# FFN gate and up as 2 by 2 blocks in seven products, inner features in chunks of 6, partial sums through DRAM

## The chip, the core and the metric

The kernel runs on one NeuronCore of a Trainium2 chip, as one launch. The metric is the time of that launch on the device in microseconds (us); of several runs the median is given.

## What is computed

A bidirectional encoder of two layers with a width of 1024 over 256 + 512 = 768 tokens, all in float32. Each layer has three token mixers (SSD, GLA, attention) with gates, an output projection and a residual, and then a gated FFN with 2816 inner features. The change is in the FFN and just ahead of it:

```python
def _layer(x, ...):
    h = _rmsnorm(x, norm1_w)
    proj = h @ w_in          # 12 parts: z, xbc, dt, gla q/k/v/..., attention q/k/v, gates
    ...
    merged = (g[:, :, 0] * (o_ssd @ w_br_ssd)
              + g[:, :, 1] * (o_gla @ w_br_gla)
              + g[:, :, 2] * (o_att @ w_br_attn))
    x = x + merged @ w_out
    h2 = _rmsnorm(x, norm2_w)
    gate, up = _split(h2 @ w_ffn_in, (D_FF, D_FF))
    return x + (jax.nn.silu(gate) * up) @ w_ffn_out
```

## The kernel before

Activations lie transposed: a tile has 128 features in the partitions and all T = 768 tokens in the columns; 8 such tiles are the width of 1024. Float32 precision comes from two parts of each operand: `hi`, rounded by ScalarE to the matmul type fp32r, and `lo`, the rest, by a subtraction. A product is three matmuls, hi x hi, hi x lo and lo x hi. Each weight unit of 512 columns (4 blocks of 128 x 128) is loaded by a DMA on SyncE's queue and split by `wunit` (L617): `hi` on ScalarE, `lo` on the engine `lo_eng`, which is VectorE from the SSD output projection to the end of the layer and GpSimd elsewhere. There are 3 buffers for raw units and 5 each for `hi` and `lo`.

`gemm_a` (L628) makes a block of 128 output features for all tokens: for each of the `kt` input blocks it runs the three products on two halves of HT = 384 tokens, so 6 matmuls for each input block and 48 for a width of 1024. The last input block comes after all the others, so that its activations may come late. The sum stands in a PSUM tile of two banks, of which there are two.

The FFN (L924 to L966) goes through 22 blocks of 128 inner features, in chunks of 8, 8 and 6 (`FF_CHUNKS`, L27). For block j it runs `gemm_a` for the gate ("fg"), multiplies by the row's rstd `r2`, applies Silu, runs `gemm_a` for up ("fu"), multiplies, and splits the result into `hid` (hi and lo). After a chunk the down projection "fo" runs `gemm_a` over the chunk's blocks for each of the 8 output blocks m and adds into `xa[m]`, which stays in SBUF from the first chunk to the last. In the last layer the last block goes through `finish` (L968) in two token halves, with the final norm.

Ahead of the FFN (L885 to L921): SSD output times z gate gives `yz` (tiles `ea`, two buffers, and `ld`, one). Six of the eight "g0" gate projections run early (`early_gate`, L1015) and go through DRAM, the last two inside `gate_branch` (L1023). The output projection "wo" (L913) adds the residual and makes `x2`, split into hi and lo.

The order of instructions is written out ahead of time: `Plan.schedule` (L450) is a list scheduler with costs that keeps each engine's stream in one fixed order. An operation recorded under `first()` goes ahead of the others that are ready. Operations of GpSimd, and those of VectorE that touch SBUF alone, are planned so that they exclude each other (`op.port`, L349). SBUF beyond the fixed tiles is cut into cells that the phases of a layer share in turn (`phase`, L603). All instructions are emitted on one line, L574, so the profile's groups go by operation and shape.

## Time and profile before

| | us |
|---|---|
| median of 3 runs | 3123.14 |
| lowest and highest | 3118.91, 3123.22 |
| the profiled execution | 3119.5 |
| its span in the profile | 3117.7 |

The profile names engines PE (TensorE matmuls), PEld (weight loads), DVE (VectorE), ACT (ScalarE), POOL (GpSimd) and SPq (SyncE's queue of DMA issues). base_S and cell are SBUF, base_P is PSUM, wts the weights and d_x, d_z, d_g and the like tensors in DRAM.

A group of instructions shows engine, operation, output <- inputs, shapes and count, then busy time in us and the mean of one in ns, then the idle time of the engine just before them with what ended it. A timeline line shows the start, the duration, the engine and the operation, and in brackets the idle time before it. A window shows for its stretch the busy time (and count) of PE, PEld, DVE, ACT and POOL in us, then PE's granted clock as a share of the full one, the share of the DMA engines and GB/s.

The FFN of layer 0 runs from about 1016 to 1564 us, that of layer 1 from about 2552 to 3101 us.

### The profile page before, as it was taken

Reading aid. Unit: us, or ns where it says so; the run is one execution under the profiler, and the core shown is the slowest. Engines: PE = TensorE matmul, PEld = TensorE weight load, DVE = VectorE, ACT = ScalarE, POOL = GpSimd, SP = SyncE. Lnnn points to the kernel's source line nnn. Section 1 sums busy time; section 2 is a strip of 40 time slices with the busy share of each in tenths; the row PEclk is TensorE's granted clock in tenths of the full one; section 3 lists DMA queues with packets and bytes.
Section 4 is the critical chain, followed back from the end, with each engine's and each line's share of the span. In section 5 each row is a group of like instructions: output and inputs, shape, how many; then the busy total and the mean of one; then the engine's idle time right before and its main releaser. Section 6 shows DMA issues by size and latency. Waiting matters only on the chain.

```text
span 3117.7 us, 46591 instructions
## 1 busy us (share of the span) xinstructions
PE 3041.2 (98%) x18160; PEld 2983.5 (96%) x18160; DVE 1606.6 (52%) x2737; ACT 1205.3 (39%) x2109; POOL 992.1 (32%) x972
## 2 busy tenths in 40 slices
PE   8999999999999999999999999999999999999998
PEld 7989989999899999999999899999998999999998
DVE  4766576856533333333447656776765333333233
ACT  4666454433323221212346755543333232122123
POOL 4533555655252000000164244556543410000002
PEclk8999999999999999999999999999999999999999
DMA  3233223444545222222222332334335452222222
GB/s 108 61 79 114 90 88 110 127 114 112 173 134 178 66 61 65 65 61 65 89 76 70 77 120 85 98 110 131 118 99 182 128 165 65 61 65 64 62 61 68
DMA packets 200012, 301.32 MB, mean 97 GB/s; under 512 B 17584, under 2 KB 90672, under 8 KB 199792
## 3 DMA queue, kind: packets, MB, share of 16 engines
q1 hardware_dynamic: 199792, 298.35, 31.8%
q8 instruction: 143, 2.34, 0.3%
q14 instruction: 77, 0.63, 0.1%
HBM read 246.18 MB, written 52.10 MB: 96 GB/s over the span
## 4 chain that ended last, share of the span: by engine, by line
PE 62%; DVE 3%; ACT 1%; DMA 0%; issue 0%; POOL 0%; DVEq 0%; ACTq 0%; POOLq 0%
PE base_P L574 62%; DVE cell L574 3%; ACT cell L574 1%; DVE base_S L574 0%; DMA base_S<-wts 0%; ACT L574 0%; ACT base_S L574 0%; DMA base_S<-d_z 0%; DMA d_g<-base_S 0%; POOL cell L574 0%; DVEq L1669 0%; POOL base_S L574 0%; DVEq L574 0%; ACTq L574 0%; POOLq L574 0%
## 5 line engine op out<-in xcount | busy, mean ns | idle before, releaser
L574 PE MATMUL base_P<-base_S 128*128 128x384 f32 (+3 forms) x12452 | 2262.1, 334 | 14.0 <-DVE base_S L574 9.6
L574 PEld LDWEIGHTS base_P<-base_S 128*128 128x128 f32 x12452 | 2103.6, 189 | 25.0 <-DVE base_S L574 12.1
L574 ACT ACTIVATE base_S<-base_S 128x512 fp32r<-128x512 f32 (+6 forms) x830 | 549.9, 668 | 1285.6 <-PE base_P L574 862.0
L574 POOL TENSOR_TENSOR cell<-cell,base_S 128x256 f32<-128x256 f32 (+3 forms) x164 | 185.9, 1144 | 1334.1 <-ACT base_S L574 1280.9
L574 PE MATMUL base_P<-cell,base_S 128*128 128x384 f32 x3136 | 577.9, 339 | 14.4 <-ACT cell L574 8.2
L574 DVE TENSOR_TENSOR base_S<-base_S,base_S 128x512 fp32r<-128x512 f32 x360 | 262.9, 730 | 627.1 <-issue 448.2
L574 PEld LDWEIGHTS base_P<-cell,base_S 128*128 128x128 f32 x3136 | 553.1, 189 | 16.9 <-ACT cell L574 8.8
L574 POOL TENSOR_TENSOR base_S<-base_S,base_S 128x512 fp32r<-128x512 f32 (+1 forms) x272 | 369.0, 1359 | 450.0 <-ACT base_S L574 185.2
L574 PE MATMUL base_P<-cell,cell 128*128 128x256 f32 (+3 forms) x1568 | 307.3, 322 | 21.5 <-ACT cell L574 13.3
L574 PEld LDWEIGHTS base_P<-cell,cell 128*128 128x128 f32 x1568 | 238.0, 191 | 45.7 <-ACT cell L574 18.3
L574 DVE TENSOR_TENSOR base_S<-base_P,base_S 128x768 f32<-128x768 f32 (+1 forms) x212 | 170.4, 804 | 212.9 <-PE base_P L574 212.2
L574 DVE TENSOR_TENSOR cell<-base_P,cell 64x128 f32<-64x128 f32 (+5 forms) x385 | 201.8, 527 | 125.4 <-PE base_P L574 85.9
L574 ACT ACTIVATE cell<-base_P 128x256 f32<-128x256 f32 (+5 forms) x344 | 148.1, 441 | 156.9 <-PE base_P L574 143.6
L574 POOL TENSOR_TENSOR cell<-cell,cell 128x256 f32<-128x256 f32 (+6 forms) x244 | 180.5, 753 | 86.2 <-DVE cell L574 49.6
L574 ACT ACTIVATE cell<-cell 128x768 f32<-128x768 f32 (+9 forms) x228 | 132.8, 608 | 145.3 <-DVE cell L574 140.4
L574 PE MATMUL base_P<-base_S,cell 128*128 128x128 f32 (+2 forms) x908 | 153.3, 276 | 15.8 <-DVE cell L574 10.0
L574 DVE SCALAR_TENSOR_TENSOR cell<-cell,base_S,cell 128x770 f32<-128x770 f32 x128 | 140.3, 1096 | 40.4 <-ACT cell L574 36.8
L574 PEld LDWEIGHTS base_P<-base_S,cell 128*128 128x128 f32 x908 | 113.8, 150 | 32.8 <-DVE cell L574 12.4
L574 ACT ACT_TABLE_LOAD x105 | 134.7, 1283 | 8.7 <-DMA cell<-xT 5.2
L574 DVE TENSOR_TENSOR cell<-base_P,base_S 128x256 f32<-128x256 f32 (+1 forms) x136 | 67.2, 512 | 98.8 <-PE base_P L574 97.8
L574 DVE TENSOR_TENSOR cell<-cell,base_S 128x1024 f32<-128x1024 f32 (+3 forms) x85 | 100.2, 1200 | 14.9 <-ACT base_S L574 9.2
L574 DVE TENSOR_TENSOR cell<-cell,cell 128x256 f32<-128x256 f32 (+4 forms) x134 | 92.2, 701 | 24.9 <-ACT cell L574 23.9
(59 smaller groups left out, 1248.2 us busy)
## 6 DMA issues: line engine op xcount, KB each, us to landing
base_S<-wts SPq DMA_DIRECT2D x584, 256.0 KB, 2.6
cell<-d_cs SPq DMA_DIRECT2D x96, 256.0 KB, 4.8
d_part<-base_S SPq DMA_DIRECT2D x32, 384.0 KB, 2.6
base_S<-d_part SPq DMA_DIRECT2D x32, 384.0 KB, 3.4
base_S<-wts SPq DMA_DIRECT2D x32, 272.0 KB, 2.7
d_z<-base_S SPq DMA_DIRECT2D x16, 384.0 KB, 2.6
d_y<-cell SPq DMA_DIRECT2D x48, 128.0 KB, 3.2
base_S<-d_y SPq DMA_DIRECT2D x16, 384.0 KB, 3.5
```

Of the source, the lines that this page charges most:

```text
L574: f(*[real(x) for x in op.args], **{k: real(x) for k, x in op.kw.items()})
```

## The change

The gate and up weights of one block j are taken as a 2 by 2 matrix of blocks: rows are gate and up (128 features each), columns are the lower and upper half of the 1024 inputs. The activations are a 2 by 2 matrix too: rows are the input halves, columns the even and the odd blocks of 128 tokens (384 tokens each). The four results (gate and up, even and odd) come from seven products of sums of such blocks (Strassen's method in Winograd's form) instead of eight products. `right_sums` makes the activations' seven operands once a layer, `left_sums` the weights' seven for each j, with four sums; `gate_up` runs the products and adds up their results out of PSUM. For the first j of a layer the first four products run three of their four input blocks before the last.

Chunks are now 6, 6, 6 and 4 blocks. A chunk's result is added to `d_x2` in DRAM: load, add, store for each output block, where `xa[m]` stayed in SBUF. Seven of the activations' sums for each of four input blocks and the hidden blocks take the space. All eight "g0" gate projections run early; `yz` loads and the residual loads alternate between two tiles; "wo" blocks come in the order 0, 4, 1, 5, 2, 6, 3, 7.

```diff
-FF_CHUNKS = ((0, 8), (8, 8), (16, 6))
+FF_CHUNKS = ((0, 6), (6, 6), (12, 6), (18, 4))
...
-        early = [("z", m) for m in range(8)] + [("g0", m) for m in range(6)]
+        early = [("z", m) for m in range(8)] + [("g0", m) for m in range(8)]
...
-            y = self.ev.tile([P, T], F32, tag="ld")
+            y = self.ev.tile([P, T], F32, tag=("ld", "sn")[m % 2])
...
+        before = self.mp
+        self.phase()
+        for m in (0, 4, 1, 5, 2, 6, 3, 7):
             ps = self.gemm_a([(l, "wo", m, 0), (l, "wo", m, 1)], mg)
-            x = self.ev.tile([P, T], F32, tag="ld")
-            self.sp.dma_start(x, self.xsrc[m])
+            with self.first():
+                x = self.ev.tile([P, T], F32, tag="sn" if m < 4 else "ld")
+                self.sp.dma_start(x, self.xsrc[m])
             self.dve.scalar_tensor_tensor(out=x, in0=ps, scalar=0.5, in1=x, op0=ALU.mult, op1=ALU.add)
             self.sp.dma_start(self.d_x2[m], x)
-            x2.append(self.split(x, (self.op, self.op), "op", "op", wcol=self.prm(C_N2 + m)))
-            self.sumsq(x, acc, False)
+            xs = self.ev.tile([P, T], F32, tag="ea", bufs=2)
+            self.act.activation(xs, x, AF.Copy, scale=self.prm(C_N2 + m))
+            pairs.append(xs)
+            if m > 3:
+                x2.append(self.right_sums(pairs[-2], pairs[-1], len(x2)))
+            self.sumsq(x, acc, False, pool=before)
...
             for j in range(c0, c0 + n):
-                psg = self.gemm_a([(l, "fg", j, 0), (l, "fg", j, 1)], x2)
...
-                psu = self.gemm_a([(l, "fu", j, 0), (l, "fu", j, 1)], x2)
...
+                ea, eb = self.gate_up(l, j, x2, r2)
...
                 self.dve.tensor_tensor(out=ea, in0=ea, in1=eb, op=ALU.mult)
...
             for m in range(8):
+                ws = self.out_weights(l, m, c0, n)
...
+                ps = self.gemm_k(ws, hid)
+                if last and end:
+                    x = xa[m] = self.mp.tile([P, T], F32, tag=f"xa{m}")
...
+                else:
+                    x = self.mp.tile([P, T], F32, tag="xr", bufs=3)
+                self.sp.dma_start(x, self.d_x2[m])
+                self.dve.tensor_tensor(out=x, in0=ps, in1=x, op=ALU.add)
+                if not end:
+                    self.sp.dma_start(self.d_x2[m], x)
...
+    def right_sums(self, lo_half, hi_half, k):
+        b11, b12 = self.parity(lo_half)
+        b21, b22 = self.parity(hi_half)
...
+        self.dve.tensor_tensor(out=t1, in0=b12, in1=b11, op=ALU.subtract)
+        self.dve.tensor_tensor(out=t2, in0=b22, in1=t1, op=ALU.subtract)
+        out = [self.piece(x, 7 * k + i) for i, x in enumerate((b11, b21, t2))]
+
+        self.dve.tensor_tensor(out=b12, in0=b22, in1=b12, op=ALU.subtract)
+        out += [self.piece(x, 7 * k + 3 + i) for i, x in enumerate((b12, t1, b22))]
+        self.dve.tensor_tensor(out=b21, in0=b21, in1=t2, op=ALU.subtract)
+        out.append(self.piece(b21, 7 * k + 6))
+        return out
...
+    def left_sums(self, l, j):
...
+        P_ = {k: getattr(self, v) for k, v in dict(d="dve", p="pool").items()}
+        e = [P_[c] for c in "dppdddpdpdd"]
+        with self.first():
+            here = (self.wp, "raw", 3) if j == 0 else (self.mp, "sr", 5)
+            a11 = raw("fg", 0, self.wp, "raw", 3)
+            w1 = self.wsplit(a11, eng=e[0])
+            a21 = raw("fu", 0, *here)
+            a22 = raw("fu", 1, *here)
...
+                a12 = raw("fg", 1, self.wp, "raw", 3)
+                w2 = self.wsplit(a12, eng=e[4])
+            e[1].tensor_tensor(out=s1, in0=a21, in1=a22, op=ALU.add)
+            e[2].tensor_tensor(out=s2, in0=s1, in1=a11, op=ALU.subtract)
+            w6 = self.wsplit(s2, eng=e[3])
+            e[6].tensor_tensor(out=a21, in0=a11, in1=a21, op=ALU.subtract)
+            w7 = self.wsplit(a21, eng=e[7])
...
+            w5 = self.wsplit(s1, eng=e[5])
+            e[8].tensor_tensor(out=s2, in0=a12, in1=s2, op=ALU.subtract)
+            w3 = self.wsplit(s2, eng=e[9])
+            w4 = self.wsplit(a22, eng=e[10])
+        return w1, w2, w6, w7, w5, w3, w4
+
+    def gate_up(self, l, j, x2, r2):
+        w = self.left_sums(l, j)
...
+        def product(i, ps, ks=range(4)):
+            for wi, ai in ((0, 0), (0, 1), (1, 0)):
+                for k in ks:
+                    self.pe.matmul(ps, lhsT=w[i][wi][:, k * P:(k + 1) * P], rhs=x2[k][i][:, ai, :],
+                                   start=(k == wi == ai == 0), stop=(k == 3 and wi == 1))
...
+        if j == 0:
+            rest = range(3, 4)
+            for i, ps in ((0, p1), (2, p6), (3, p7), (1, p2)):
+                product(i, ps, range(3))
+        product(0, p1, rest)
+        with self.first():
+            self.act.activation(u2, v(p1), AF.Copy)
+        product(1, p2, rest)
+        add(g_e, p2, u2)
+        product(2, p6, rest)
+        add(u2, p6, u2)
+        product(3, p7, rest)
+        add(u3, p7, u2)
+        p5, p3 = banks()
+        product(4, p5)
+        add(u_o, p5, u3)
+        add(u2, p5, u2)
+        product(5, p3)
+        add(g_o, p3, u2)
+        p4, _ = banks()
+        product(6, p4)
+        add(u_e, p4, u3)
+        self.dve.tensor_tensor(out=ea, in0=ea, in1=r2, op=ALU.mult)
+        self.act.activation(ea, ea, AF.Silu)
+        self.dve.tensor_tensor(out=eb, in0=eb, in1=r2, op=ALU.mult)
+        return ea, eb
```

`piece` splits an operand with 384 columns into hi (ScalarE) and lo (VectorE), `wsplit` a weight operand with 512. `out_weights` loads the down projection's units, or halves of them where a chunk ends inside a unit, and `gemm_k` is `gemm_a` over them. The PSUM tiles of `banks` hold two products, one in each bank; `add` runs on VectorE under `first()`.

## Rows read from the trace of the kernel before

**Rows 1.** The page's first part: TensorE's busy time, share of the span and instructions.

```profile
PE 3041.2 (98%) x18160; PEld 2983.5 (96%) x18160; DVE 1606.6 (52%) x2737; ACT 1205.3 (39%) x2109; POOL 992.1 (32%) x972
```

**Rows 2.** The chain that ended last, its two longest pieces: start, us, what.

```profile
1015.86 590.60 PE base_P L574 x3462
...
2407.52 692.82 PE base_P L574 x3974
```

**Rows 3.** Windows by stage, inside an FFN and ahead of the second FFN.

```profile
1100.00:1150.00 50.00, 50.00 (x288) 50.00 (x287) 18.97 (x24) 12.34 (x18) 0.00 (x0) 1.00 0.22 64
2500.00:2550.00 50.00, 50.00 (x288) 50.00 (x287) 19.38 (x24) 17.57 (x24) 10.21 (x6) 1.00 0.60 205
```

**Rows 4.** Groups of instructions by form, 1050 to 1500 us, inside layer 0's FFN.

```profile
L574 PE MATMUL base_P<-base_S 128*128 128x384 f32 x1807 | 316.3, 336 | 0.0
...
L574 DVE TENSOR_TENSOR base_S<-base_S,base_S 128x512 fp32r<-128x512 f32 x108 | 74.2, 687 | 206.5 <-issue 167.7 <-PE base_P L574 38.9
L574 ACT ACTIVATE base_S<-base_S 128x512 fp32r<-128x512 f32 x107 | 67.3, 629 | 301.9 <-PE base_P L574 220.9 <-issue 81.0
L574 DVE TENSOR_TENSOR base_S<-base_P,base_S 128x768 f32<-128x768 f32 x38 | 36.4, 958 | 51.5 <-PE base_P L574 51.5
L574 DVE TENSOR_TENSOR base_S<-base_S 128x768 f32<-128x768 f32 x19 | 18.1, 952 | 0.0
...
L574 ACT ACTIVATE base_S<-base_S 128x768 f32<-128x768 f32 x19 | 16.1, 847 | 12.6 <-DVE base_S L574 12.6
```

**Rows 5.** Timeline of TensorE: a projection by tokens, and the last output block.

```profile
59.81 6.19 PE L574 MATMUL base_P<-base_S 128*128 128x272 f32 x48
...
3091.78 5.24 PE L574 MATMUL base_P<-cell,base_S 128*128 128x384 f32 x29
```

**Rows 6.** Groups by form over the whole span: VectorE, 384 columns from PSUM.

```profile
L574 DVE TENSOR_TENSOR cell<-base_P,cell 128x384 f32<-128x384 f32 x2 | 1.1, 558 | 6.4 <-PE base_P L574 6.4
```

**Rows 7.** Timeline, from the last chunk's gate and up to its down projection, layer 0.

```profile
1513.56 50.59 PE L574 MATMUL base_P<-cell,base_S 128*128 128x384 f32 x288
...
1513.76 0.96 DVE L574 TENSOR_TENSOR base_S<-base_P,base_S 128x768 f32<-128x768 f32 x1 [2.30 <-PE base_P L574]
1514.63 0.69 DVE L574 TENSOR_TENSOR base_S<-base_S,base_S 128x512 fp32r<-128x512 f32 x1
1515.23 0.95 DVE L574 TENSOR_TENSOR base_S<-base_S 128x768 f32<-128x768 f32 x1
...
1517.10 0.96 DVE L574 TENSOR_TENSOR cell<-base_S,cell 128x768 fp32r<-128x768 f32 x1 [0.91 <-ACT cell L574]
```

**Rows 8.** Timeline, GpSimd alone, beside VectorE on SBUF, and beside VectorE on PSUM.

```profile
1556.56 1.29 POOL L574 TENSOR_TENSOR base_S<-base_S,base_S 128x512 fp32r<-128x512 f32 x1 [0.29 <-ACT cell L574]
...
840.86 1.96 POOL L574 TENSOR_TENSOR cell<-cell,base_S 128x768 f32<-128x768 f32 x1 [4.63 <-ACT base_S L574]
841.02 2.35 DVE L574 TENSOR_TENSOR base_S<-base_S,base_S 128x512 fp32r<-128x512 f32 x1
...
868.07 4.08 POOL L574 TENSOR_TENSOR base_S<-base_S,cell 128x768 f32<-128x768 f32 x2 [7.19 <-DVE cell L574]
...
870.39 0.94 DVE L574 SCALAR_TENSOR_TENSOR base_S<-base_P,base_S 128x768 f32<-128x768 f32 x1
```

**Rows 9.** Timeline ahead of the SSD output projection, layer 1.

```profile
2379.83 0.94 DVE L574 TENSOR_TENSOR base_S<-base_P,base_S 128x768 f32<-128x768 f32 x1
...
2380.83 4.47 PE L574 MATMUL base_P<-cell,base_S 128*128 128x384 f32 x24 [2.11 <-DVE base_S L574]
...
2381.68 0.32 SPq L574 DMA_DIRECT2D d_g<-base_S  x1
...
2384.33 1.32 SPq L574 DMA_DIRECT2D base_S<-d_z  x2
...
2389.26 0.62 PE L574 MATMUL base_P<-cell,base_S 128*128 128x384 f32 x2 [3.96 <-ACT cell L574]
...
2390.31 8.26 PE L574 MATMUL base_P<-cell,base_S 128*128 128x384 f32 x38 [0.44 <-DVE cell L574]
```

More of the change, by code (lines that the diff above doesn't have):

```diff
@@ L687, in split, with sumsq @@
         return hi, lo
-    def sumsq(self, src, accs, last, eng=None, which=0):
+    def sumsq(self, src, accs, last, eng=None, which=0, pool=None):
         if last:
@@ new lines, in layer @@
+                if last and end:
+                    x = xa[m] = self.mp.tile([P, T], F32, tag=f"xa{m}")
+                    if m == 0:
+                        xa[7] = self.mp.tile([P, T], F32, tag="xa7")
+                        self.sp.dma_start(xa[7], self.d_x2[7])
+                else:
+                    x = self.mp.tile([P, T], F32, tag="xr", bufs=3)
[3 more added lines that the diff above has]
+                    self.sp.dma_start(self.d_x2[m], x)
+                elif not last:
+                    self.sp.dma_start(self.d_x[m], x)
+                    self.l = l + 1
+                    x1.append(self.split(x, (self.op, self.op), "op", "op", wcol=self.prm(C_N1 + m)))
+                    self.l = l
+                    self.sumsq(x, acc, False)
+                else:
+                    self.sumsq(x, acc, False)
+                    self.act.activation(x, x, AF.Copy, scale=self.prm(C_FN + m))
@@ new lines, in parity, with piece @@
+    @staticmethod
+    def parity(v):
+        w = v.rearrange("p (b x c) -> p x b c", x=2, c=P)
+        return w[:, 0], w[:, 1]
+    def piece(self, src, i):
+        if i < 12:
+            if i % 2 == 0:
+                self.two = self.mp.tile([P, 2, 2, HT], F32R, tag="pc", bufs=6)
+            t = self.two[:, i % 2]
+        else:
+            t = self.op.tile([P, 2, HT], F32R, tag="op")
+        hi, lo = (t[:, x].rearrange("p (b c) -> p b c", c=P) for x in range(2))
+        self.act.activation(hi, src, AF.Copy)
+        self.dve.tensor_tensor(out=lo, in0=src, in1=hi.bitcast(F32), op=ALU.subtract)
+        return t
@@ new lines, in out_weights, with gemm_k @@
+    def out_weights(self, l, m, c0, n):
+        ws, c = [], c0
+        while c < c0 + n:
+            e = min(c // 4 * 4 + 4, c0 + n)
+            u = self.wunit(l, "fo", m, c // 4, cols=(c % 4 * P, (c % 4 + e - c) * P))
+            ws += [[x[:, i * P:(i + 1) * P] for x in u] for i in range(e - c)]
+            c = e
+        return ws
+    def gemm_k(self, ws, acts, halves=((0, 1),)):
+        ps = self.pg.tile([P, 1024], F32, tag="g")
+        kt = len(acts)
+        for hs, ks in [(hs, ks) for hs in halves for ks in (range(kt - 1), range(kt - 1, kt))]:
+            for wi, ais in ((0, (0, 1)), (1, (0,))):
+                for k in ks:
+                    for ai in ais:
+                        for h in hs:
+                            self.pe.matmul(ps[:, P + h * HT:P + (h + 1) * HT], lhsT=ws[k][wi],
+                                           rhs=acts[k][ai][:, h * HT:(h + 1) * HT],
+                                           start=(k == wi == ai == 0), stop=(k == kt - 1 and wi == 1))
+        return ps[:, P:P + T]
```

95 lines of the change are left out of this document (57 added, 38 removed).

## The prediction

> **What bounds the kernel now.** I read the profile page first. The shares by engine say TensorE: 98% of the span in 18,160 matmuls, VectorE 52% [rows 1]. A share is an average, so next comes the chain of work that ended last: its two longest pieces, 590.60 and 692.82 us, are matmuls alone, and they lie over the two FFNs [rows 2]. Then the windows by stage: inside an FFN 288 matmuls run in every 50 us, PE is busy for all 50, and the granted clock is 1.00, the 2.4 GHz level [rows 3]. So an FFN costs 50/288 = 0.1736 us for each matmul with 384 columns and nothing else, while VectorE is used for 19 of 50 us and GpSimd not at all. What removes matmuls there shortens the time one for one, until another engine or a hand-over becomes later than PE.
>
> **What it removes.** Before, a block j of 128 inner features takes gate and up, each 8 input blocks x 3 products of hi and lo x 2 token halves = 48 matmuls, so 96. After, it takes 7 products x 4 x 3 = 84 matmuls of the same 384 columns. 12 x 22 blocks x 2 layers = 528 fewer. The down projection keeps 22 x 8 x 6 = 1056 a layer. If the rate stays, 528 x 0.1736 = **91.7 us less**.
>
> Does the rate stay? The new order changes the weight block at every matmul and writes one PSUM bank in a row. One matmul lasts 0.336 us from start to end, and they overlap [rows 4]. A projection that already changes its stationary block each time runs 48 matmuls of 272 columns in 6.19 us, so (6.19 - 0.34)/47 = 0.125 each; the last FFN output, in one bank at a time, runs 29 in 5.24 us, (5.24 - 0.34)/28 = 0.175 each [rows 5]. 272 columns at 2.4 GHz are 0.113 us and 384 are 0.160, so the surplus is 0.012 and 0.015, beside 0.014 now. I take 0.1736; the bounds are 0.172 and 0.175, which over 3696 new matmuls is 6 us either way.
>
> **What it adds in a block.** A block now lasts 84 x 0.1736 = 14.6 us on PE, where it had 16.7. The other engines get more:
> - ScalarE: 7 hi copies instead of 4 at 0.63, one copy from PSUM below 0.63, one Silu and one hi copy at 0.85 [rows 4]: 4.4 + 0.6 + 1.9 = 6.9 of 14.6 us. It fits.
> - VectorE: 7 lo subtractions at 0.69, 7 additions from PSUM at 0.56 [rows 6], 4 long operations at 0.95 [rows 4]: 4.8 + 3.9 + 3.8 = 12.5 us. These durations overlap by a little: behind a 0.96 operation the next starts after 0.87, behind a 0.69 one after 0.60 [rows 7]. By starts it is 7 x 0.60 + 7 x 0.47 + 4 x 0.87 = 11.0 us, three quarters of the block.
> - GpSimd: 4 sums of 512 columns at 1.29 [rows 8] = 5.2 us, where it had nothing.
>
> VectorE and GpSimd are not independent. At 840.86 GpSimd begins an addition of 1.96 us; a VectorE subtraction of two SBUF operands begins at 841.02 and takes 2.35 us instead of 0.69, ending 0.55 after GpSimd's end. A VectorE operation that reads PSUM, at 870.39 inside GpSimd's 4.08, takes its usual 0.94 [rows 8]. So the operations with both operands in SBUF wait for one another: 4.2 + 3.5 + 5.2 = 12.9 of 14.6 us if they only exclude each other, with the PSUM additions beside GpSimd; 11.0 + 5.2 = 16.2 to 12.5 + 5.2 = 17.7 if every GpSimd sum holds VectorE up.
>
> I take the first, since the waits have room. There are 5 slots for split weights, so the split for a product may come four products (4 x 2.08 = 8.3 us) before its use. A VectorE operation held up by a sum of 1.29 delays those behind it, the PSUM additions among them; a bank is wanted again after 3.6 us or more, but for the pair of the fifth and sixth products, wanted 2.08 us after the sixth ends. There a delay of 1.29 + 0.56 + 0.6 can cost up to 0.4 us. Bounds for a block: 0 to 3.1 (17.7 - 14.6); I take 0.1, **+4 us** over 44 blocks.
>
> The Trainium skill ("Perfetto Trace Analysis", Optimizing Scalar/DVE Operations) says that GpSimd shares an SBUF port with the Vector engine, so that moving work between the two might not help; "SBUF — State Buffer", Who interferes with whom, calls it an exclusive lock for instructions with two SBUF inputs. The row at 841.02 agrees. By that rule the split of the new sums over both engines is worth little, and the block goes by the 16.2 to 17.7 above, priced below as a rival.
>
> **What it adds between stages.** The last block of a chunk is handed to the down projection: PSUM sum, times rstd, times gate, hi, lo. Before, that chain took from 1513.56, where the next group's matmuls begin, to 1518.06 = 4.5 us [rows 7]; now an addition of 0.56 stands ahead: 5.1. It is covered by the matmuls of the other k: 30 x 0.1736 = 5.2 us in chunks of 6 and 18 x 0.1736 = 3.1 in the chunk of 4 (a chunk of 8 had 7.3). Splits for the next weights and the next block's GpSimd sums run ahead of that chain: two more splits and a sum are 2.5 us. So 0 to 2.5 us at each of 6 hand-overs (I take 0.7, near the low end, because the low end is the row of before that was fully hidden) and 1.5 to 4 at the 2 short ones (1.8): **+8 us**, bounds 3 to 23.
>
> After the output projection, VectorE makes for each pair of blocks 4 sums and 7 lo subtractions with 384 columns, each between 0.56 and 0.69 [rows 4, 6]: 6.2 to 7.6, with 2 residual additions and 4 weight splits 11 to 12 of the 16.7 us of 96 matmuls. Only the last pair stands out. Its first pieces need 0.96 + 0.85 + 0.6 + 0.6 = 3.0 us, the four first wanted some 5; the first block runs its other three k first, 36 x 0.1736 = 6.3 us. Then the sum of squares goes on later through the single buffer that the sums hold, and rstd with it, which PE has in its queue: 0 to 3 us a layer, I take 1.5, **+3 us**.
>
> Partial sums through DRAM: a load, an addition and a store for each of 8 blocks in each chunk. The load feeds an addition 6.2 us (36 matmuls) after the one before, with 3 buffers; a stretch that moved 205 GB/s kept PE busy for all 50 us [rows 3]. The last chunk of layer 0 has 1.0 MB in 4.2 us, 250 GB/s for 33 us, somewhat more than any row shows; layer 1 stores nothing there. The stores wait in SyncE's queue for the addition, and weight loads stand behind them; those have the buffers of one group ahead. I cost it at 0; without that cover each of 62 groups could lose 1 us.
>
> At the end the last group's halves are 2.1 us each and not 3.1, while rstd waits for GpSimd's addition to the squares behind the group before, 768 columns like the 1.96 us of [rows 8]: **+1 us**.
>
> **What it moves.** The last two gate projections (2 x 8.4 us of matmuls) go ahead of the SSD output projection. There PE waits now: 2.11 + 3.96 + 0.44 us in layer 1 [rows 9], and layer 0 repeats the pattern. The row of the gate's evacuation, its store and the load behind it shows why: two tiles carry both gates and SSD output, and the load at 2384.33 follows the store at 2381.68 [rows 9]. The new matmuls stand between; but two PSUM buffers and the same two tiles let PE run ahead only by two gates. Of 2 x 6.5 = 13 us I take 9 back (bounds 0 and 13): **-9 us**. Prefetching the residual by the boosted load and a second tile is costed at nothing.
>
> **Sum.** The profiled execution was 3119.5 us (span 3117.7). 3119.5 - 91.7 - 9 + 4 + 8 + 3 + 1 = 3034.8. The median of the runs stands 3.6 above the profiled one; some of that applies, so **3036 us**, 0.972 of before. With all small terms at their good end 3119.5 - 92 - 13 + 3 = 3018; with the second-to-worst (0.5 a block, 15 for hand-overs, 6 at the start, nothing back) 3119.5 - 92 + 22 + 15 + 6 + 1 = 3072.
>
> **Rivals.**
> 1. VectorE and GpSimd set the pace in part: a block lasts about 15.6 us, since the static order of the two engines doesn't fit the real waits. 3034.8 + 44 x 0.9 = 3075. For it: 12.9 of 14.6 us leaves little. Against: four products of lead. 17%, between 3060 and 3110.
> 2. The exclusion is complete: each sum holds VectorE up for its full length, and the block is 17.7 us. It decides from 16.7, the block of before: 44 x (17.7 - 16.7) = +44, with 12 for the stages and nothing given back 3119.5 + 44 + 12 = **3176, slower**. This is the mechanism of the skill's lock. For it: the 2.35 at 841.02. Against: it needs VectorE to stand behind all four sums, though it has over 3 us idle and 3.3 us of PSUM work in a block. 7%; 1% more for a clock that falls in new gaps.
> 3. The same with 16.2 and part of the stage costs: 3119.5 - 44 x 0.5 + 20 = 3118, no change. 4%.
> 4. The change doesn't do what it says only if the rate falls with the new order; [rows 5] leave at most 6 us, inside the range.
>
> **How the numbers follow.** Forecast 71%, 3012 to 3060; rival 1 17%, rival 2 8%, rival 3 4%. A range from 3012 to 3085 holds the forecast and over half of rival 1, 81%. About 0.2% is what a measurement of this kernel can tell from no change. Faster 0.88, same 0.04, slower 0.08.
>
> **What would show it.** Right: 17,632 matmuls or so; windows inside the FFN with PE at 50 of 50 us and 288 matmuls, VectorE near 40, GpSimd near 17; gaps of 1 to 2 us before the last k of a chunk's first down projection; fewer gaps ahead of the SSD projection. Rival 1 or 2: PE idle inside blocks, released by VectorE, its 512-column subtractions well over 0.69 on average, and fewer than 280 matmuls in 50 us. A matmul interval above 0.18 with PE busy would make the first term wrong.

## The result, and the profile after

The changed kernel takes **3040.98 us**, median of 4 runs (3039.69 to 3043.3); the kernel before took 3122.3 beside it. The ratio is 0.974 with an interval of 0.9725 to 0.976: 81 us less by the medians. The forecast was 3036. Once more on another occasion, with the later experiments: 3039.8 us, ratio 0.974 [0.973, 0.975]. The profiled execution took 3039.69 us, its span is 3037.9.

The page's first part, the answer to [rows 1]:

```profile
PE 2958.3 (97%) x17632; PEld 2898.0 (95%) x17632; DVE 1986.4 (65%) x3297; ACT 1340.0 (44%) x2374; POOL 1266.7 (42%) x1148
```

528 matmuls fewer, as counted. TensorE lost 83 us of busy time, less than 528 matmuls are worth, and the end came 80 us earlier. The chain that ended last, to compare with [rows 2] (start, us, what):

```profile
1026.52 540.33 PE base_P L574 x3164
...
2520.68 491.33 PE base_P L574 x2811
```

It is still TensorE alone over both FFNs. The windows say how fast: 1050 to 1100 is gate and up, 1250 to 1300 the down projection with its partial sums, 1050 to 1450 the middle of layer 0's FFN.

```profile
1050.00:1100.00 50.00, 50.00 (x288) 50.00 (x287) 45.44 (x62) 21.68 (x34) 21.40 (x13) 1.00 0.20 59
...
1250.00:1300.00 50.00, 50.00 (x288) 50.00 (x287) 18.09 (x27) 10.38 (x18) 8.05 (x6) 1.00 0.60 192
...
1050.00:1450.00 400.00, 400.00 (x2288) 400.00 (x2287) 277.04 (x379) 135.56 (x217) 107.14 (x69) 1.00 0.37 116
```

The same 288 in 50 us and the same full clock as in [rows 3]: 400/2288 = 0.1748 us for a matmul, no gap in 400 us, although VectorE is now used for 45 of 50 us in gate and up, and the down projection moves 192 GB/s. The operations by form, 1050 to 1250 us (columns as in [rows 4]):

```profile
L574 DVE TENSOR_TENSOR base_S<-cell,base_S 128x512 fp32r<-128x512 f32 x46 | 39.1, 850 | 4.1 <-PE base_P L574 3.4 <-ACT base_S L574 0.6
...
L574 POOL TENSOR_TENSOR cell<-base_S,cell 128x512 f32<-128x512 f32 x18 | 27.7, 1538 | 40.0 <-DVE base_S L574 40.0
...
L574 DVE TENSOR_TENSOR base_S<-base_P,cell 128x384 f32<-128x384 f32 x40 | 22.1, 552 | 11.5 <-PE base_P L574 9.3 <-ACT base_S L574 1.9
```

A lo split of 512 columns takes 850 ns where [rows 4] had 687, and a GpSimd sum 1538 where [rows 8] had 1.29 us: the two do hold one another up (e1 below takes GpSimd's part away). An addition out of PSUM takes 552, as [rows 6]. TensorE doesn't notice.

So the rest of the account lies in the two stretches ahead of the FFN. I take windows of 50 us that begin 65 us and 215 us after the same event, a group of matmuls that ends the attention part (at 774.31 and 2310.59 us before, at 774.70 and 2269.13 after). The first holds the SSD output projection, the second the start of the FFN. Undisturbed they would hold 288 or a few more. Before, layer 0 and layer 1 of each:

```profile
839.31:889.31 50.00, 42.80 (x240) 41.53 (x240) 24.50 (x25) 17.74 (x24) 25.20 (x13) 0.97 0.51 160
2375.59:2425.59 50.00, 42.81 (x241) 41.52 (x241) 24.43 (x26) 17.93 (x24) 25.88 (x14) 0.97 0.52 162
989.31:1039.31 50.00, 49.07 (x290) 48.75 (x289) 20.59 (x25) 17.63 (x24) 5.98 (x3) 1.00 0.49 166
2525.59:2575.59 50.00, 50.00 (x297) 50.00 (x296) 18.86 (x25) 17.39 (x24) 6.29 (x3) 1.00 0.49 164
```

and after:

```profile
839.70:889.70 50.00, 44.90 (x251) 44.26 (x249) 24.75 (x26) 17.55 (x24) 17.56 (x9) 0.93 0.48 158
2334.13:2384.13 50.00, 46.77 (x267) 46.46 (x267) 23.03 (x25) 18.53 (x25) 20.86 (x11) 0.97 0.50 164
989.70:1039.70 50.00, 44.53 (x246) 42.28 (x245) 35.26 (x51) 23.73 (x40) 22.35 (x15) 0.97 0.35 114
2484.13:2534.13 50.00, 44.18 (x244) 41.90 (x243) 36.55 (x51) 22.55 (x37) 21.85 (x14) 0.97 0.35 111
```

I count matmuls and not idle time, because behind some of the gaps the matmuls go on at a lower clock (PEclk 0.93 and 0.97 in these windows), so that a gap can cost more than its length. Around the SSD output projection 481 became 518: 37 x 0.1748 = 6.5 us regained (of the waits in [rows 9], 2.11 + 3.96 + 0.44 us, layer 1 keeps one of 3.23, at 2348.87). At the start of the FFN 587 became 490: 97 x 0.1748 = 17.0 us lost. The end is read from the evacuation of output block 6 in the last layer, before and after:

```profile
3092.50 0.96 DVE L574 TENSOR_TENSOR cell<-base_P,cell 128x768 f32<-128x768 f32 x1 [5.35 <-PE base_P L574]
...
3012.04 0.96 DVE L574 TENSOR_TENSOR cell<-base_P,cell 128x768 f32<-128x768 f32 x1 [3.23 <-PE base_P L574]
```

From there to the end of the span (3117.72 and 3037.88) it is 25.2 us before and 25.8 after, with 12 matmuls (2.1 us) fewer behind it: 2.7 lost. Together: -528 x 0.1748 - 6.5 + 17.0 + 2.7 = **-79.1 us**, where the profiled executions differ by 3119.5 - 3039.7 = 79.8. The counts of one program differ by up to 10 matmuls (1.7 us) in a pair of windows from one execution to another (e7 below), so part of this close agreement is luck.

The start of layer 0's FFN, line by line, shows where the 17 us begin:

```profile
1009.29 1.52 POOL L574 TENSOR_TENSOR base_S<-base_S 128x512 f32<-128x512 f32 x1 [1.11 <-DVE base_S L574]
1009.59 1.63 DVE L574 TENSOR_TENSOR base_S<-base_S 128x384 f32<-128x384 f32 x1
...
1011.75 0.80 PE L574 MATMUL base_P<-base_S 128*128 128x384 f32 x3 [1.45 <-DVE base_S L574]
...
1012.46 3.83 DVE L574 TENSOR_TENSOR base_S<-base_S,base_S 128x512 fp32r<-128x512 f32 x4 [0.77 <-ACT base_S L574]
1016.22 1.01 DVE L574 TENSOR_TENSOR base_S<-base_S,base_S 128x384 fp32r<-128x384 f32 x2
...
1016.82 0.61 PE L574 MATMUL base_P<-base_S 128*128 128x384 f32 x2 [2.04 <-DVE base_S L574]
...
1026.52 1.50 PE L574 MATMUL base_P<-base_S,cell 128*128 128x1 f32 x12 [0.54 <-POOL cell L574]
...
1029.78 0.84 PE L574 MATMUL base_P<-cell,base_S 128*128 128x384 f32 x2
...
1030.42 0.84 PE L574 MATMUL base_P<-base_S 128*128 128x384 f32 x2
```

From 1004.85 us, the evacuation of the last "wo" block, to 1026.6 VectorE is busy for 19.1 of 21.8 us. A sum of 384 columns at 1009.59 takes 1.63 us, beside a GpSimd sum that runs from 1009.29. Four splits of weights stand in VectorE's queue from 1012.46 and take 3.83 us; behind them, at 1016.22, come two lo pieces of activations with 384 columns, for which TensorE waits 2.04 us, until 1016.82. With two behind ScalarE and GpSimd it is five waits, 1.45 + 2.04 + 0.47 + 0.95 + 0.54 = 5.45 us; layer 1 has 1.43 + 2.05 + 1.55 + 0.79 = 5.82. Before there was one of 0.93 in both layers together. Then comes the second part of the price: at 1029.78 and 1030.42 two matmuls take 0.64 us from start to start, 0.32 each, which is 384 columns at 1.2 GHz, and the granted clock says the same:

```profile
1029.50:1031.00 1.50, 1.50 (x6) 1.50 (x5) 0.00 (x0) 0.63 (x1) 1.20 (x1) 0.50 0.00 0
```

A mean of 0.97 over 50 us, as the windows after have it, is some 1.5 us lost in each layer. The longer waits (10.3 us) and the clock (3) make some 13 of the 17 us; the rest isn't traced, and up to 1.7 of it is the scatter of the counts.

### The profile page after: what moved, and what is told of

The parts are those of the page before. It is cut to its first block, busy times and chain, and to the rows that moved or that the text cites. A ratio compares the mean times of both kernels' runs of the same rounds, so it can differ in the third digit from the quotient of the medians.

```text
span 3037.9 us, 47386 instructions
## 1 busy us (share of the span) xinstructions
PE 2958.3 (97%) x17632; PEld 2898.0 (95%) x17632; DVE 1986.4 (65%) x3297; ACT 1340.0 (44%) x2374; POOL 1266.7 (42%) x1148
## 4 chain that ended last, share of the span: by engine, by line
PE 87%; DVE 7%; ACT 3%; DMA 2%; issue 1%; POOL 1%; SPq 0%; another core or an unknown queue 0%; DVEq 0%; ACTq 0%; POOLq 0%
PE base_P L574 87%; DVE cell L574 6%; DVE base_S L574 2%; ACT cell L574 1%; ACT base_S L574 1%; ACT L574 0%; DMA base_S<-d_z 0%; DMA d_x<-base_S 0%; POOL cell L574 0%; POOL base_S L574 0%; DMA base_S<-wts 0%; DMA d_y<-cell 0%; DMA d_g<-base_S 0%; DMA cell<-xT 0%; DMA base_S<-rope 0%
## 5 line engine op out<-in xcount | busy, mean ns | idle before, releaser
L574 PEld LDWEIGHTS base_P<-base_S 128*128 128x128 f32 x11876 | 2024.8, 190 | 39.1 <-DVE base_S L574 25.2
L574 PE MATMUL base_P<-cell,base_S 128*128 128x384 f32 x3184 | 744.8, 338 | 0.0
L574 DVE TENSOR_TENSOR base_S<-base_S,base_S 128x512 fp32r<-128x512 f32 (+3 forms) x378 | 303.1, 806 | 251.0 <-issue 198.0
L574 DVE TENSOR_TENSOR cell<-base_P,cell 128x384 f32<-128x384 f32 (+6 forms) x533 | 289.4, 545 | 130.1 <-PE base_P L574 82.1
L574 POOL TENSOR_TENSOR cell<-cell,cell 128x256 f32<-128x256 f32 (+7 forms) x286 | 252.7, 894 | 250.2 <-DVE base_S L574 116.8
L574 ACT ACTIVATE base_S<-cell 128x512 fp32r<-128x512 f32 (+5 forms) x345 | 188.8, 547 | 331.4 <-PE base_P L574 261.3
L574 PE MATMUL base_P<-cell,cell 128*128 128x256 f32 (+3 forms) x1568 | 307.0, 322 | 18.9 <-ACT cell L574 10.5
L574 POOL TENSOR_TENSOR cell<-base_S,cell 128x512 f32<-128x512 f32 x84 | 125.6, 1495 | 217.4 <-DVE base_S L574 217.4
L574 DVE TENSOR_TENSOR base_S<-base_S 128x768 f32<-128x768 f32 (+3 forms) x184 | 189.9, 1033 | 16.9 <-DMA base_S<-d_z 12.4
L574 DVE TENSOR_TENSOR base_S<-cell,base_S 128x512 fp32r<-128x512 f32 (+1 forms) x214 | 180.1, 842 | 25.8 <-PE base_P L574 20.5
L574 DVE SCALAR_TENSOR_TENSOR cell<-cell,base_S,cell 128x770 f32<-128x770 f32 x128 | 140.3, 1096 | 40.6 <-ACT cell L574 37.1
L574 DVE TENSOR_TENSOR base_S<-base_P,base_S 128x768 f32<-128x768 f32 (+1 forms) x124 | 86.2, 695 | 91.0 <-PE base_P L574 89.8
```

The costliest lines, as they stand in the source:

```text
L574: f(*[real(x) for x in op.args], **{k: real(x) for k, x in op.kw.items()})
```

## The experiments

In the text below e1 to e12 are short for the runs, as their expectations name them. e1, e2, e5 and e6 ran together; so did e3, e4, e7 and e8, then e9 to e11; e12 ran by itself. Where a run is set against the changed kernel of another occasion, both the difference of the medians and that of the ratios (0.001 is 3.1 us) are given as a span; the changed kernel is then that of e7. The 95% interval of a ratio is 0.0013 to 0.002 either way, so a difference of less than some 6 us between two versions isn't clear of noise by the ratios. The counts of matmuls are from one execution each.

### GpSimd's sums on VectorE (e1)

```diff
-        e = [P_[c] for c in "dppdddpdpdd"]
+        e = [P_[c] for c in "ddddddddddd"]
```

> The changed kernel with all four weight sums of a block on VectorE, GpSimd idle there. Theory (PE sets the pace inside the blocks, the exclusion between VectorE and GpSimd is hidden by the four products of lead): the block stays 84 x 0.175 = 14.7 us, PE busy in every window inside the FFN, 3041 us within 5; somewhat less (3 to 6) if the start of the FFN, where PE waits, gains from the missing exclusion. Rival 1 (the exclusion sets the pace in part): 15 to 40 us faster. Rival by busy times (VectorE 12.5 + 4 x 0.69 = 15.3 us a block): 0.6 x 44 = 26 us slower.

Measured: 3032.95 us, ratio 0.9721 [0.970, 0.974] against 0.974: 6 to 7 us less, just past the theory's 3 to 6 and hardly clear of noise; both rivals (15 to 40 faster, 26 slower) fall. The start of the FFN holds 258 and 249 matmuls, 17 more than after (3.0 us), in an execution that is the longest of its four (3037.72; the others 3029.68 to 3035.51). The middle of the FFN of this kernel, first the window, then the lo splits by form:

```profile
1050.00:1450.00 400.00, 400.00 (x2289) 400.00 (x2288) 281.74 (x445) 135.81 (x218) 0.00 (x0) 1.00 0.39 116
...
L574 DVE TENSOR_TENSOR base_S<-cell,base_S 128x512 fp32r<-128x512 f32 x85 | 58.1, 683 | 9.1 <-PE base_P L574 7.3 <-ACT base_S L574 1.8
```

Without GpSimd beside it the split takes 683 ns again, where the changed kernel's took 850. TensorE runs 2289 matmuls without a gap, with all of GpSimd's work there on VectorE. VectorE executes 66 instructions more and is busy for only 4.7 us more (277.04 to 281.74). Run undisturbed, 66 at 0.687 [rows 4] are 45.3 us; so by this estimate the 69 GpSimd operations had cost VectorE 45.3 - 4.7 = 40.6 us of waiting, about 0.6 each. The split over two engines bought nearly nothing. The Trainium skill ("SBUF — State Buffer", Who interferes with whom) states that VectorE instructions with two SBUF inputs and GpSimd instructions that read SBUF lock each other out; this run agrees: the work that kept GpSimd busy for 107.14 us adds only 4.7 to VectorE's time. But the block doesn't become longer, as the prediction's rivals 1 and 2 had it: in the changed kernel VectorE's waits fit into its slack.

### All sums and splits on GpSimd (e2)

```diff
-        e = [P_[c] for c in "dppdddpdpdd"]
+        e = [P_[c] for c in "ppppppppppp"]
```

> The changed kernel with all four weight sums and all seven lo subtractions of a block on GpSimd: 11 x 1.29 = 14.2 us there. Theory (VectorE's operations on two SBUF operands and GpSimd's exclude each other): 14.2 + 4 x 0.87 = 17.7 us a block against 14.7 on PE, so PE must wait inside the blocks; 40 us slower than 3041 if the down projections between the chunks take up part of the backlog, up to 3.0 x 44 = 132 if they take none. Rival (the engines only share, nothing is exclusive): 14.2 is under 14.7, 3041 within 8.

Measured: 3074.64 us, ratio 0.986 [0.984, 0.988], 35 to 37 us more than the changed kernel, a little under the theory's 40; the rival (3041 within 8) falls. Windows (one in gate and up, then the middle of the FFN):

```profile
1200.00:1250.00 50.00, 48.39 (x272) 46.88 (x270) 32.07 (x36) 17.79 (x31) 47.66 (x33) 1.00 0.21 58
1050.00:1450.00 400.00, 393.17 (x2229) 388.68 (x2228) 204.26 (x254) 125.36 (x212) 258.66 (x179) 1.00 0.38 113
```

and the first matmul group of layer 0 that waits for rstd:

```profile
1031.27 2.72 PE L574 MATMUL base_P<-base_S,cell 128*128 128x1 f32 x12 [9.26 <-POOL cell L574]
```

Now an engine does set the pace: GpSimd is busy for 47.66 of 50 us and TensorE makes 272 matmuls instead of 288. Over 400 us that is 59 matmuls or 10.3 us; at each start some 9.3 us more stand in one gap (9.26, 9.35 in layer 1). This is what rival 1 would have looked like. With 11 operations per block on GpSimd it happens, with 4 it doesn't; no run lies between.

### The last pair's sums left out (e6)

```diff
-                x2.append(self.right_sums(pairs[-2], pairs[-1], len(x2)))
+                x2.append(self.right_sums(pairs[-2], pairs[-1], len(x2)) if len(x2) < 3 else x2[2])
```

The sums and splits of the last pair of "wo" blocks aren't computed; the products use the third pair's.

> The changed kernel without the sums and splits of the last pair of activation blocks in each layer: the products use the third pair's operands in their place, so that part of the FFN is not computed. Theory (PE waits at the start of each FFN, 5.5 us in layer 0 and 5.8 in layer 1 with a lower clock behind it, since VectorE's queue of some 10 us after the last output block is longer than the 6.3 us of cover): most of it goes, 9 to 14 us faster than 3041. Rival (the start waits for the weights, or for the rstd alone, whose matmuls stand in PE's queue): no more than 3 us faster.

Measured: 3022.83 us, ratio 0.969 [0.968, 0.970], 15 to 17 us less, a little past the theory's 9 to 14. The start of the FFN, both layers:

```profile
991.22:1041.22 50.00, 50.00 (x296) 50.00 (x296) 36.09 (x51) 24.09 (x38) 24.30 (x16) 1.00 0.40 125
2477.64:2527.64 50.00, 48.98 (x286) 48.05 (x285) 35.10 (x47) 22.56 (x35) 24.12 (x16) 1.00 0.42 127
```

582 matmuls, 92 more than after: 16.1 us. Without these 4 sums and 7 splits the loss at the start is gone, so it isn't the weights or rstd alone. Whether it comes from the chain itself or from what stands before it in VectorE's queue, this run doesn't tell; e11 below does in part.

### The changed kernel once more (e7), and the order at the start (e4, e11)

> The changed kernel itself once more, on the same chip as the three runs beside it, so that each of them can be held against it and not only against the kernel before. Expected: a ratio to the kernel before of 0.972 to 0.976.

Measured: 3039.8 us, ratio 0.974 [0.973, 0.975]. Its windows hold 245 + 265 and 245 + 235 matmuls, so the same program scatters by up to 9 in one window and by 10 in the sum of two.

The first block's products whole, not three quarters first:

```diff
-        if j == 0:
+        if False:
             rest = range(3, 4)
```

> Undoes one part of the change: the first block of gate and up runs its products whole, in the order of all other blocks, and no longer the first three input blocks of four products ahead of the last one. Theory (the start of the FFN is bound by VectorE's queue, which is full from the last output projection on): the order costs at most its cover, the products wait at the first piece of the last pair instead of after 36 matmuls, 36 x 0.174 = 6.3 us a layer of cover goes, but part of it is lost already; 4 to 10 us more in all, ratio 0.9755 to 0.9775. Rival (VectorE is not what is late, the cover decides alone): all of it, 12.5 us or more, ratio 0.978 or above. Second rival (the cover is worth nothing since the sums come too late either way): within 2 us.

Measured: 3043.59 us, ratio 0.976 [0.975, 0.977], 3.8 us more; 225 + 227 matmuls at the start, 38 fewer than in the first profile of the changed kernel (6.6 us), 28 fewer than in the one beside it (4.9). That is just under the theory's 4 to 10, and neither rival: the 36 matmuls drawn ahead are 6.3 us of TensorE's work a layer, but only 2 to 3 us of time. What VectorE still has in its queue is late with or without them.

The sums recorded ahead of other ready work:

```diff
             if m > 3:
-                x2.append(self.right_sums(pairs[-2], pairs[-1], len(x2)))
+                with self.first():
+                    x2.append(self.right_sums(pairs[-2], pairs[-1], len(x2)))
```

> Another part of the reordered version alone: the sums of the activations are recorded as work that goes ahead of other ready work. Theory: the start of the FFN is late because these sums and their lo parts stand behind splits of the next weights in VectorE's queue. Undisturbed the 50 us around the start hold 288 or more matmuls; the changed kernel has 246 and 244 there, the reordered one 288 and 280. If the order alone is enough: 275 or more in each, (288 - 245) x 2 x 0.174 = 10 to 15 us less than the changed kernel, ratio 0.969 to 0.971. Rival: VectorE has too much to do there in any order, and the weights' sums have to leave GpSimd's lock too: 260 or fewer, 2 to 5 us less, ratio about 0.973.

Measured: 3029.84 us, ratio 0.972 [0.9705, 0.973], 7 to 10 us less than the changed kernel. The start of the FFN:

```profile
989.63:1039.63 50.00, 47.54 (x268) 46.48 (x267) 36.84 (x57) 25.81 (x43) 22.71 (x16) 0.97 0.39 119
2480.51:2530.51 50.00, 45.38 (x260) 43.34 (x260) 38.22 (x55) 23.49 (x38) 23.64 (x15) 1.00 0.36 111
```

38 matmuls more than after, 6.6 us. That lies between theory and rival: by this count the order in VectorE's queue is worth about 40% of what the start lost. In e8, below, where most of GpSimd's work goes to VectorE as well, 78 come back.

### Ahead of the SSD output projection (e3, e9, e12, e10)

Six early gates, one tile for the loads, and both:

```diff
-        early = [("z", m) for m in range(8)] + [("g0", m) for m in range(8)]
+        early = [("z", m) for m in range(8)] + [("g0", m) for m in range(6)]
...
-            mg.append(self.gate_branch("g0", "bs", m, yz, self.d_part2[m], None, rs, self.d_g0[m] if m < 8 else None))
+            mg.append(self.gate_branch("g0", "bs", m, yz, self.d_part2[m], None, rs, self.d_g0[m] if m < 6 else None))
```

> Undoes one part of the change: again six of the eight g0 gate projections run early, the last two inside the gate branch. The prediction gave the two moved gates 9 us (bounds 0 and 13). Theory: the stall ahead of the SSD output projection comes back; reading the gaps of both traces I expect about 6 us more than the changed kernel (3 to 9), a ratio near 0.976, and TensorE gaps of about 6 to 7 us a layer just ahead of that projection in place of about 5. Rival: the gaps only move with the gates (the same store, load and two tiles limit TensorE wherever they stand): within 2 us of the changed kernel.

Measured: 3041.05 us, ratio 0.975 [0.974, 0.9765], 1.3 us more than the changed kernel, inside the scatter; 255 + 260 = 515 matmuls around that projection. That the moved gates as such gave the gain falls; the rival holds.

```diff
-            y = self.ev.tile([P, T], F32, tag=("ld", "sn")[m % 2])
+            y = self.ev.tile([P, T], F32, tag="ld")
```

> Undoes one part of the change: ahead of the SSD output projection the loads of the SSD output go into one tile again instead of two in turn; all eight gates stay early. The 50 us around that projection hold 240 and 241 matmuls in the kernel before (full would be 288), 251 and 267 with the change, and 255 and 260 with six early gates and two tiles. Theory: it is the second tile that gave the change its gain there, and not the two moved gates (the prediction gave the gates 9 us and the tile nothing). Then one tile gives the stall of before back: about 240 matmuls in those 50 us of each layer, some 4 to 7 us more than the changed kernel, ratio 0.9755 to 0.9765. Rival: the gates did it, and either of the two is enough: 250 or more matmuls there, within 2 us of the changed kernel.

Measured: 3043.47 us, ratio 0.976 [0.975, 0.9775]; 265 + 243 = 508 matmuls, as many as in e7 (510). Not the 480 of the theory: the count speaks for its rival, that either of the two is enough. The time, 4 to 7 us more and hardly clear of noise, speaks for the theory, though the execution that was profiled is the shortest of its four (3040.7; the others 3043.4 to 3045.9). So both were undone:

> Undoes both parts ahead of the SSD output projection: six early gates and one tile for the loads of the SSD output, as in the kernel before. In the 50 us around that projection the kernel before has 240 and 241 matmuls (481 in both layers), the changed kernel 518 and 510 in two profiles, six gates with two tiles 515, eight gates with one tile 508. Theory: the six gates and the one tile each leave most of the gain because either is enough to let TensorE run on; with both undone the stall of before is back: 475 to 490 matmuls, 4 to 6 us more than the changed kernel. Rival: neither made the gain; it comes from something else of the change (the residual's loads taken ahead, the new order of cells in SBUF) and stays: 500 or more, within 2 us of the changed kernel.

Measured: 3046.96 us, ratio 0.978 [0.976, 0.979], 7 to 11 us more than the changed kernel, where 4 to 6 was expected.

```profile
838.49:888.49 50.00, 42.29 (x238) 40.94 (x238) 23.92 (x26) 17.94 (x24) 25.00 (x13) 0.97 0.52 161
2331.72:2381.72 50.00, 41.84 (x227) 40.41 (x227) 25.23 (x25) 16.95 (x23) 23.67 (x12) 0.93 0.49 154
```

465 matmuls: the stall of [rows 9] is back, somewhat deeper than before (481) and than expected (475 to 490); why deeper isn't shown. Two more gates or a second tile: either alone keeps most of the gain by the count of matmuls. By the time the tile may be worth more than the gates (1.3 us lost without the two gates, 4 to 7 without the tile), but that difference isn't clear of noise. And where the gates stand matters more than their number:

```diff
-            if m % 2 and early:
+            if m in (1, 2, 3, 4, 5, 6) and early:
                 self.early_gate(*early.pop(0))
```

> One part of the reordered version alone: the early gates that stand between the eight steps ahead of the SSD output projection are placed behind the steps 1 to 6 instead of behind 1, 3, 5 and 7. In the reordered version the 50 us around that projection held 286 matmuls in layer 0 and 256 in layer 1, where the changed kernel has 251 and 267. Theory: the place of the gates decides that stall in layer 0, (286 - 251) x 0.174 = 6 us, and does nothing in layer 1: 4 to 7 us less than the changed kernel, ratio 0.9715 to 0.973. Rival: the gain there came from VectorE and GpSimd being used otherwise, not from the gates: within 2 us.

Measured: 3032.08 us, ratio 0.972 [0.971, 0.974], 5 to 8 us less (the theory had 4 to 7).

```profile
840.51:890.51 50.00, 49.04 (x287) 48.40 (x287) 27.59 (x28) 19.11 (x26) 19.23 (x10) 1.00 0.59 186
2329.39:2379.39 50.00, 49.59 (x292) 49.24 (x292) 28.51 (x28) 19.22 (x26) 19.55 (x11) 1.00 0.59 188
```

The stall is gone in both layers (61 matmuls more, 10.7 us; the start of the FFN has 472 in this profile, 18 fewer, 3.1 us). I had expected nothing in layer 1.

### Chunks of 4 (e5)

```diff
-FF_CHUNKS = ((0, 6), (6, 6), (12, 6), (18, 4))
+FF_CHUNKS = ((0, 4), (4, 4), (8, 4), (12, 4), (16, 4), (20, 2))
```

> The changed kernel with chunks of 4, 4, 4, 4, 4 and 2 blocks: two more hand-overs and two more rounds of partial sums through DRAM a layer, the same matmuls. Theory (the planned order fills a hand-over with the matmuls of two output blocks, 2 x 18 x 0.175 = 6.3 us for a chunk of 4, over the chain of 4.8 to 5.1; DRAM is hidden): nothing at the chunks of 4, some 3 us at each chunk of 2 (2 x 6 x 0.175 = 2.1 of cover): 3041 + 6, within 5. The step of the prediction (cover of one output block, 1.8 at each short hand-over): 10 x 1.8 + 2 x 4 - 4 = 22 slower. Rival (the partial sums at 1.0 MB in 4.2 us are not hidden): up to 1 us for each of 94 groups, 50 to 90 slower, with PE waiting for loads of the partial sums.

Measured: 3058.24 us, ratio 0.981 [0.979, 0.982], 18 to 21 us more. The theory (6 within 5) missed; the number is near the 22 of the prediction's step, but not for its reason: at no hand-over to a chunk of 4 does TensorE wait, in either layer. The hand-over to the chunk of 2 costs 1.70 us in each. Behind its start, all gaps of layer 0's FFN lie in the chunk of 2:

```profile
1510.00 10.60 PE L574 MATMUL base_P<-base_S 128*128 128x384 f32 x48 [1.70 <-ACT base_S L574]
1523.21 4.44 PE L574 MATMUL base_P<-base_S 128*128 128x384 f32 x24 [2.62 <-DVE cell L574]
1528.92 2.33 PE L574 MATMUL base_P<-base_S 128*128 128x384 f32 x12 [1.27 <-DVE cell L574]
1533.85 2.35 PE L574 MATMUL base_P<-base_S 128*128 128x384 f32 x12 [2.59 <-DVE cell L574]
```

VectorE in the same stretch:

```profile
1517.63 4.56 DVE L574 SCALAR_TENSOR_TENSOR base_S<-cell,base_S,base_S 128x768 fp32r<-128x768 f32 x2
...
1527.82 0.96 DVE L574 TENSOR_TENSOR cell<-base_P,cell 128x768 f32<-128x768 f32 x1 [1.88 <-DMA cell<-d_x]
```

An output block lasts 2.1 us on TensorE there, and two things that were hidden come out: the lo parts of the next layer's input, two in 4.56 us, and the load of the partial sum, for which VectorE waits 1.88 us. In layer 1 TensorE waits 5.52 us at 3034.96 for the last rstd, which stands behind GpSimd's sums of squares; these come every 2.8 us where an output block takes 2.1. The waits behind the start are 8.2 us in layer 0 and 7.6 in layer 1, most of the 18 to 21. So the partial sums in DRAM cost nothing with 24 matmuls to an output block, and do cost with 12.

### A version put together from this (e8)

The sums first; weights' sums and splits on VectorE except for the first block of a layer; gates spread over six places; in the last layer the sum of squares of output block 6 on VectorE:

```diff
-            if m % 2 and early:
+            if m in (1, 2, 3, 4, 5, 6) and early:
...
+                with self.first():
+                    x2.append(self.right_sums(pairs[-2], pairs[-1], len(x2)))
...
-                    self.sumsq(x, acc, False)
+                    self.sumsq(x, acc, False, self.dve if m == 6 else None)
...
-        e = [P_[c] for c in "dppdddpdpdd"]
+        e = [P_[c] for c in ("dppdddpdpdd" if j == 0 else "ddddddddddd")]
```

> A version built on what the earlier runs showed: the weights' sums and their splits all on VectorE except for the first block of a layer, the activations' sums of the start ahead of the other work that is ready (so ahead of the next weights' splits), the sum of squares of the last but one output block of the last layer on VectorE, and the early gates of the stretch ahead of the SSD output projection spread over six places instead of four. Theory: the first gives 5 us (as measured when the sums went to VectorE), the order at the start gives back 5 to 9 of the 11 us of gaps there, the others 1 to 3: 9 to 15 us less than the changed kernel, ratio 0.969 to 0.971. Rival (VectorE's queue is full at the start, so an order within it gains nothing): 4 to 6 us less, ratio 0.9725, with gaps of 9 us or more left over the two starts.

Measured: **3012.2 us**, ratio 0.966 [0.965, 0.9675]; 27.6 us less than the changed kernel beside it, almost twice the upper end of what I expected. The profiled execution is the longest of its four (3017.25; the others 3011.6 to 3012.3). Its windows, SSD projection and then start, both layers of each:

```profile
839.56:889.56 50.00, 48.79 (x286) 48.14 (x285) 27.36 (x28) 19.15 (x26) 18.98 (x10) 1.00 0.58 182
2317.34:2367.34 50.00, 48.27 (x256) 47.64 (x255) 26.50 (x26) 17.73 (x24) 14.89 (x8) 0.90 0.50 156
989.56:1039.56 50.00, 49.61 (x288) 48.29 (x287) 41.97 (x71) 25.49 (x41) 15.30 (x8) 1.00 0.42 125
2467.34:2517.34 50.00, 48.19 (x280) 46.86 (x279) 40.54 (x69) 24.79 (x42) 11.61 (x7) 1.00 0.38 117
```

78 matmuls more at the start (13.6 us), 24 more ahead of the SSD projection (4.2 us), and the end takes 24.7 us, 1.1 less: 18.9 of the 22.4 us by which the profiled executions differ. The parts alone (e1, e11, e10) gave 6 to 7, 7 to 10 and 5 to 8 us, which is 18 to 25. Part of the miss was in the gates, to which I had given 1 to 3 with the end; another part is that the two edits at the start do more together, 78 matmuls, than alone, 17 + 38. Some 3 us of the profiled difference lie outside these windows and aren't explained.

## Why the prediction was right, and where it wasn't

**The main term** (-91.7) held: 528 matmuls fewer at an unchanged rate. 0.1736 was a little short, since 288 in 50 us is a coarse count; over 400 us it is 0.1748, and the term -92.3. Bank order and changed weights cost nothing, as [rows 5] had said.

**The block** (+4, bounds 0 to 136 over 44 blocks): 0. VectorE and GpSimd do hold each other up, and more than I took: VectorE is busy for 45 of 50 us where I had forecast near 40, GpSimd for 21 where I had 17. But TensorE has no gap in 400 us. The step "the waits have room" was right, and the 0.1 for a late bank too careful; that it is the four products of lead that give the room is argued, since no run changed them. Rivals 1, 2 and 3 are refuted with this amount of GpSimd work, and e2 shows that rival 1 comes true with more of it. Rival 4 falls with the rate, 0.1748. In the sum for ScalarE two operations at 0.85 are 1.7 us and not 1.9; nothing hangs on it.

**Hand-overs** (+8): 0. Failed step: "It is covered by the matmuls of the other k". The end of the chunk of 4 in layer 0:

```profile
1490.81 0.56 DVE L574 TENSOR_TENSOR base_S<-base_P,cell 128x384 f32<-128x384 f32 x1 [0.34 <-PE base_P L574]
...
1494.55 0.96 DVE L574 TENSOR_TENSOR base_S<-base_S,base_S 128x768 fp32r<-128x768 f32 x1 [0.46 <-ACT base_S L574]
...
1497.49 0.95 DVE L574 TENSOR_TENSOR cell<-base_P,cell 128x768 f32<-128x768 f32 x1
...
1499.19 0.96 DVE L574 TENSOR_TENSOR cell<-base_P,cell 128x768 f32<-128x768 f32 x1 [0.42 <-PE base_P L574]
```

The chain was rightly sized: 1490.81 to 1495.51 is 4.7 us, where I had 5.1. The cover wasn't. The first two output blocks leave PSUM from 1497.49 and 1499.19, 1.7 us apart, where a block of 24 matmuls lasts 4.2: TensorE had run the ready inputs of both before the last input of either. With two PSUM tiles and a written-out order the cover is 2 x 18 x 0.175 = 6.3 us and not 3.1. e5 bears it out: no wait at any hand-over to a chunk of 4, and 1.70 us at the chunk of 2, where the cover is 2.1. The code showed this to whoever asked what else TensorE can run; I looked at one `gemm_a` only.

**Start of the FFN** (+3, bounds 0 to 6): 17.0, the largest miss. Mechanism and place were named, the last pair and rstd behind it; the size failed in the step that gave the first four pieces "some 5" us against 6.3 of cover. It counted the last pair's own operations by undisturbed durations. Not in it were the splits of the next weights in the same queue (four from 1012.46; e11, about 7 us by the count), the GpSimd sums beside them (1.63 us for a sum that takes 0.55; e1, 3 us by the count), and the lower clock behind the waits (some 3 us in both layers). The counts scatter by 1.7 us, and e8 shows that the first two don't simply add up.

**The moved gates** (-9): -6.5, inside the bounds, but put down to one edit of two. Failed step: "Prefetching the residual by the boosted load and a second tile is costed at nothing", for the tile in the loads ahead of that projection. I gave everything to the gates; by the counts of e3, e9 and e12 the tile alone holds the gain as well as the gates alone do, and only without both is it gone. e10 shows that the gates' place would have given the rest.

**Partial sums** (0): right for 6 and 4 blocks. **The end** (+1): +2.7; in e8, with the sum of squares of output block 6 on VectorE, it is 1.1 less, so the addition on GpSimd that the prediction named is part of it. The rest stays open.

The terms besides the first came to +7 by forecast and to -6.5 + 17.0 + 2.7 = +13.2 by measurement. Of that difference of 6.2 the first term gives 0.6 back: 5.6, near the 4.9 by which the profiled execution lies above 3034.8. Two terms too high (12 us together) paid for most of the one that was 14 too low. The size of the main term was foreseen; that the total came as near as 5 us is luck.

## What to carry to other kernels

A fast product method pays where TensorE is the bound and the extra sums find time beside it; count them per engine, then look for the place where they have no cover. Here that was the first block after the operands are made, and not the steady state. There, size the queue of the engine that makes the operands with everything that is in it, the next stage's prefetches too. Where two engines hold each other up, as here, the second adds little: put the sums on the faster one unless it is full.

## What the hardware showed that I hadn't expected

Small gaps can be dear. In the reordered version, ahead of layer 1's SSD projection, TensorE waits 1.29 us and 0.44 us and then runs 12 matmuls of one column:

```profile
2345.84 0.62 PE L574 MATMUL base_P<-cell,base_S 128*128 128x384 f32 x2 [1.29 <-ACT cell L574]
2346.90 2.88 PE L574 MATMUL base_P<-cell,base_S 128*128 128x384 f32 x10 [0.44 <-DVE cell L574]
```

The windows around it:

```profile
2340.00:2350.00 10.00, 8.27 (x41) 7.64 (x41) 6.25 (x6) 4.95 (x6) 1.94 (x1) 0.89 0.76 237
2350.00:2360.00 10.00, 10.00 (x44) 10.00 (x45) 1.22 (x3) 0.90 (x2) 0.70 (x1) 0.60 0.19 65
```

In the second window it is busy throughout, at a granted clock of 0.60, with 44 matmuls instead of 58. Not every such gap does this: in e10, waits of 0.52 and 0.44 us at the same place in layer 0 left the granted clock of the window at 1.00. A profile in which "PE is busy" can hide this; the count of matmuls doesn't. And GpSimd relieved VectorE hardly at all: 69 operations in 400 us saved it 4.7 us.
